# Gate weights split earlier, branch B's chunks moved to another bank ring, branch A's rings swapped

## The chip, the cores and the metric

The kernel runs on one core of a Trainium2 chip. The metric is device time in microseconds (us) of one execution; lower is better. Three runs of the kernel before gave 1930.98, 1931.53 and 1932.75 us, with a median of 1931.53 us. One further execution was taken with the hardware profiler; its own time was 1933.68 us, and the span from its first to its last instruction is 1931.9 us.

## The reference

One layer of an encoder over 1024 tokens of width 1024, all in float32:

```python
h = h + 0.5 * swiglu(rms_norm(h, ffn1_norm), ffn1_w_gate, ffn1_w_up, ffn1_w_down)
z = rms_norm(h, mix_norm) @ w_in          # 4352 columns
qa, ka, va, qb, kb, vb, ga, gb = split(z)
ya = neighbourhood_attention_2d(qa, ka, va, na_rpb)     # branch A, 8 heads
yb = windowed_gqa_sink(rope(qb), rope(kb), vb, sink)    # branch B, 8 heads on 2 key heads
merged = sigmoid(ga) * (ya @ w_branch_a) + sigmoid(gb) * (yb @ w_branch_b)
h = h + merged @ w_out
h = h + 0.5 * swiglu(rms_norm(h, ffn2_norm), ffn2_w_gate, ffn2_w_up, ffn2_w_down)
y = rms_norm(h, final_norm)
```

## The kernel before

**Arithmetic.** Every large product is made three times: each operand is split into a high part (rounded to fp32r, a cast on ScalarE, L95) and a low part (what is left, a subtraction on VectorE, L98), and TensorE adds high·high, high·low and low·high (`mm3`, L149, L151 and L153). The two feed-forward layers, most of the input projection and the output projection also use Strassen's seven products, whose combinations cost VectorE time.

**Stages in order of time.** FFN 1's hidden layer (to about 430 us), its down projection, the input projection (to about 917 us), the two attention branches with the remaining gates and the branch products in between (917 to 1207 us), the output projection (from 1207 us), and FFN 2 in the same two steps.

**PSUM.** There are eight banks of 128x512 in two rings of four, tagged `d` and `g`. `bank(tag)` takes the next free one of a ring; a matmul that opens a bank waits until the last reader of its former contents is through.

**Attention.** A loop takes 64 units (32 of branch B, then 32 of branch A), each one block of 128 queries for two heads. `scores` (L1366) takes two `d` banks, subtracts the maximum (L1382), takes the exponential (L1385) and normalises (L1389 and L1390). `turn` (L1392) transposes the probabilities on TensorE into two `d` banks (L1398) and splits them into a pair of `ws` buffers. `values` (L1405) multiplies with the values into one `g` bank, and the unit's `write` takes it out: for branch A (in `units_a`, L1340) a ScalarE copy of 64x256 (L1348), a VectorE sum of 64x256 (L1349) and two sums of 64x128 (L1352).

**What fills TensorE between units.** `filling` draws steps from a generator `filler` (L1290). Its first part is `gate` (L1197): six blocks of 128 gate columns that the projection left over (list `gates`, L945), eight steps each, two `g` banks each. The weights of a block are 512 KB, loaded and split by `load_w` (L111) at step 4 of the block before, the first block's by `gate_first` (L1102) at the end of the projection. Then comes `branch_b` (L1256): eight chunks `dc`, each four steps of `branch_mm` into two banks, whose ring alternates `d`, `g`. A chunk's gate is fetched by `fetch_gate` (L1243) into one of the two `xs` buffers one chunk ahead, opened by a tanh on ScalarE (`open_gate`, L1252), and multiplied in by VectorE (L1279), which also frees the banks. `split_y` splits the four blocks of branch B's result that the chunks multiply. Last come the first two chunks of branch A; the other six are issued by the loop after the attention, which multiplies their gates in at L1518, adds them at L1519 and forms four combinations each second chunk at L1495. `branch_a` (L1235) alternates the rings `g`, `d`, so chunk 7, the last, writes `d`. The output projection (`Down` with `n` = 4) follows on TensorE at once. Its first product P2 takes all four `d` banks at L623, and its P1 all four `g` banks at L621.

**Work behind FFN 1.** `behind_ffn1` (L739) is called after each of FFN 1's products with the number `n` of products still to come. Besides feeding the down projection, it prepares the 16 weight chunks of the two branches: `wab_fetch` (L725) loads 256 KB into a buffer of the ring `hs` (six buffers of 128x512), `wab_split` (L729, casts at L731, subtractions at L732) makes two more, and `wab_put` (L735) sends these to DRAM by POOL's queue. One chunk is taken every four products, from `n` = 80 on: fetched, split two products later, put four products later. The last put comes at `n` = 16, before the down projection uses `hs` for the bias tables.

**Key loads of branch A.** `prep_a` (L1159) is a generator drawn twice per unit that loads the queries and keys of two heads by POOL's queue, then turns the values.

**Order.** A list scheduler places the instructions of each engine; those marked `pin` keep their program order. FFN 1's first stage is ordered by hand.

Of the kernel before, what the change touches and what calls it, by code (L numbers as in the profile page):

```python
# [36 lines left out]
def trunk_kernel(ctx, tc, x, xt, n1, wg1, wu1, wd1, nm, win, rpb, sink, wa, wb, wo,  # L37
# [681 lines left out]
    wab_d = dram.tile([2 * NC8, P, 1024], F32, name="wab_d")  # L719
    cast = {}  # L720
# [4 lines left out]
    def wab_fetch(i):  # L725
        r = cast[i] = hs(F32)
        nc.sync.dma_start(r.rearrange("p (c f) -> p c f", f=P), w_cols(*((wb[0], i * P) if i < NC8 else (wa[0], a_order[i - NC8] * P))))
# [196 lines left out]
    with tc.manual_schedule(engines={E.DVE, E.Activation, E.PE, E.SP, E.Pool}):  # L924
# [17 lines left out]
    groups = [[(12, 13), (14, 15)], [(16, 17), (0, 1)], [(4, 5), (8, 9)], [(2, 3), (6, 7)], [(10, 11), (18, 19)],  # L942
              [(20, 21), (22, 23)], [(24, 25), (26, 27)]]
    NG = len(groups)
    gates = [dc for dc in [*range(8, 16), *range(8)] if 18 + dc not in sum((p for g in groups for p in g), ())]  # L945

# [154 lines left out]

    def gate_first():  # L1102
        mix["gate"] = load_w(win[0], GA + gates[0] * P, xs4())
# [55 lines left out]
    def prep_a(hp):  # L1159
# [75 lines left out]
    def branch_a(i):  # L1235

        bs = [bank("gd"[i % 2]) for _ in range(2)]
# [14 lines left out]
    def open_gate(dc):  # L1252
        r = mix["rb", dc]
        pin(nc.scalar.activation(r, r, AF.Tanh, scale=0.5))

    def branch_b():  # L1256
# [4 lines left out]
        for dc in range(NC8):  # L1261
            bs = [bank("dg"[dc % 2]) for _ in range(2)]
            mm = branch_mm(bs, mix.pop(("w", dc)), Y_B)
            for c in range(4):
                drain(mm, 1)
                yield
                if c == 0:
                    if dc == 0:
                        open_gate(0)
                    if dc + 1 < NC8:  # L1270
                        fetch_gate(dc + 1)
                elif c == 1:
# [4 lines left out]
            for n in range(2):  # L1277
                sl = slice(n * 512, (n + 1) * 512)
                nc.vector.scalar_tensor_tensor(out=merged(dc)[:, sl], in0=rb[:, sl], scalar=1.0, in1=bs[n],  # L1279
# [374 lines left out]
```

## Time and profile before

| | us |
|---|---|
| median of three runs | 1931.53 |
| lowest and highest | 1930.98, 1932.75 |
| profiled execution, its own time | 1933.68 |
| profiled execution, span | 1931.9 |
| TensorE (PE) busy in the span | 1913.6 |
| VectorE (DVE) busy | 1458.8 |
| ScalarE (ACT) busy | 947.6 |

In the profile PE stands for TensorE's matmuls, PEld for its weight loads, DVE for VectorE, ACT for ScalarE, POOL for GpSimd; SPq and POOLq are the queues that issue DMAs. L12 is line 12 of the kernel. A row of the timeline gives start, length, engine, line, operation and operands, and in brackets the idle time before it with what ended it. A row of the table by stage gives for each stretch of time the busy time and, in brackets, the number of instructions of each engine, then PEclk, the clock granted to TensorE as a share of the full one, the mean busy share of the DMA engines, and GB/s. A row of the list of waits gives who waited for whom, the total in us, the number of times and the longest. Matmuls are pipelined, so the 0.39 us of one overlaps the next; their spacing is the measure of speed.

### The profile page before, as it was taken

To read this page: it belongs to the slowest core of one execution; us is meant where nothing else is said; L and a number is where in the kernel's file an instruction comes from. 1 tells how busy PE (TensorE), PEld (TensorE's weight loads), DVE (VectorE), ACT (ScalarE), POOL (GpSimd) and SP (SyncE) were. 2 spreads that over 40 slices of the span, in tenths; PEclk is the share of its full clock that TensorE was granted. 3 is DMA by queue.
4 is the path that set the end of the run, shared out by engine and by line. 5 is a ranking of instruction groups with operands and counts; after the bars stand their busy time and mean duration, and the time that the engine had idled before them with its cause. 6 is when DMAs were issued, how large, how long until landed. Compare 5 with 4: busy or idle time off the path is not lost.

```text
span 1931.9 us, 25661 instructions
## 1 busy us (share of the span) xinstructions
PE 1913.6 (99%) x8908; PEld 1592.9 (82%) x8908; DVE 1458.8 (76%) x2559; ACT 947.6 (49%) x1846; POOL 297.4 (15%) x458
## 2 busy tenths in 40 slices
PE   9999999999999999999999999999999999999998
PEld 7888888888888888888888788788888888888886
DVE  8987766668966878656888997989676566569864
ACT  7532444444446543435898883465333333344453
POOL 0011111214400112211112101010111001005210
PEclk9999999999999999999999999999999999999999
DMA  6254555586354377834438958543422323492341
GB/s 267 94 173 166 177 177 192 171 300 241 124 172 150 108 199 239 257 107 140 128 89 216 242 198 302 175 153 120 147 96 101 130 87 105 146 353 101 113 136 67
DMA packets 161408, 321.76 MB, mean 167 GB/s; under 512 B 16384, under 2 KB 70016, under 8 KB 161280
## 3 DMA queue, kind: packets, MB, share of 16 engines
q1 hardware_dynamic: 130048, 225.21, 35.9%
q0 software_dynamic: 30512, 93.87, 14.7%
q8 instruction: 70, 1.15, 0.2%
q10 hardware_dynamic: 720, 1.05, 0.1%
q14 instruction: 58, 0.48, 0.1%
HBM read 222.04 MB, written 99.81 MB: 167 GB/s over the span
## 4 chain that ended last, share of the span: by engine, by line
PE 94%; DVE 3%; ACT 2%; issue 1%; DMA 1%; SPq 0%; POOLq 0%; POOL 0%; DVEq 0%
PE g L151 17%; PE g L149 17%; PE g L153 17%; PE d L149 12%; PE d L153 12%; PE d L151 12%; PE d L1398 2%; PE g L1417 1%; PE d L1379 1%; PE d L1380 1%; ACT fa L1385 1%; PE g L1412 1%; PE d L142 1%; ACT ws L95 1%; DVE ar L98 0%
## 5 line engine op out<-in xcount | busy, mean ns | idle before, releaser
L149 PE MATMUL g<-ar,ws 128*128 128x512 f32 x1064 | 406.8, 392 | 0.0
L151 PE MATMUL g<-ar,ws 128*128 128x512 f32 x1064 | 404.5, 390 | 0.0
L153 PE MATMUL g<-ar,ws 128*128 128x512 f32 x1064 | 404.0, 390 | 0.0
L149 PE MATMUL d<-ar,ws 128*128 128x512 f32 x784 | 303.0, 391 | 0.7 <-ACT ar L877 0.5
L151 PE MATMUL d<-ar,ws 128*128 128x512 f32 x784 | 302.0, 390 | 0.6 <-DVE ar L879 0.6
L153 PE MATMUL d<-ar,ws 128*128 128x512 f32 x784 | 301.2, 390 | 0.2 <-DVE ws L322 0.2
L153 PEld LDWEIGHTS g<-ar,ws 128*128 128x128 f32 x1064 | 199.3, 188 | 40.6
L151 PEld LDWEIGHTS g<-ar,ws 128*128 128x128 f32 x1064 | 199.4, 188 | 40.3
L322 DVE TENSOR_TENSOR ws<-raw,ws 128x512 fp32r<-128x512 f32 x222 | 152.1, 691 | 102.6 <-ACT ws L319 101.5
L149 PEld LDWEIGHTS g<-ar,ws 128*128 128x128 f32 x1064 | 197.7, 188 | 37.6 <-DVE fa L997 0.4
L319 ACT CAST ws<-raw 128x512 fp32r<-128x512 f32 x222 | 136.5, 621 | 152.2 <-PE g L153 65.0
L149 PEld LDWEIGHTS d<-ar,ws 128*128 128x128 f32 x784 | 146.9, 188 | 31.8 <-ACT ar L877 1.1
L153 PEld LDWEIGHTS d<-ar,ws 128*128 128x128 f32 x784 | 147.1, 188 | 30.9 <-DVE ws L322 0.7
L151 PEld LDWEIGHTS d<-ar,ws 128*128 128x128 f32 x784 | 147.0, 188 | 30.8 <-DVE ar L879 1.2
L95 ACT CAST ws<-raw 128x512 fp32r<-128x512 f32 (+1 forms) x103 | 66.4, 645 | 125.8 <-PE d L153 62.2
L98 DVE TENSOR_TENSOR ws<-raw,ws 128x512 fp32r<-128x512 f32 (+1 forms) x103 | 79.7, 774 | 44.3 <-ACT ws L95 44.2
L426 POOL DMA_DIRECT2D hid<-fx x91 | 49.4, 543 | 374.0 <-DVE fx L486 245.8
L98 DVE TENSOR_TENSOR ws<-ar,ws 128x512 fp32r<-128x512 f32 x114 | 93.9, 831 | 16.2 <-ACT ws L95 16.1
L95 ACT CAST ar<-raw 128x512 fp32r<-128x512 f32 (+1 forms) x81 | 54.1, 671 | 85.6 <-PE g L151 50.8
L149 PE MATMUL g<-ws,ws 128*128 128x512 f32 x232 | 90.9, 392 | 0.0
L153 PE MATMUL g<-ws,ws 128*128 128x512 f32 x232 | 90.4, 390 | 0.0
L151 PE MATMUL g<-ws,ws 128*128 128x512 f32 x232 | 90.3, 389 | 0.0
(313 smaller groups left out, 3669.8 us busy)
## 6 DMA issues: line engine op xcount, KB each, us to landing
raw<-hid SPq DMA_DIRECT2D x70, 512.0 KB
hid<-fx POOLq DMA_DIRECT2D x91, 256.0 KB, 2.6
ar<-in_ffn_w_down_dram SPq DMA_DIRECT2D x32, 512.0 KB
raw<-in_ffn_w_up_dram SPq DMA_DIRECT2D x31, 512.0 KB
raw<-in_ffn_w_gate_dram SPq DMA_DIRECT2D x27, 512.0 KB
hid<-fa POOLq DMA_DIRECT2D x51, 256.0 KB, 2.8
raw<-in_w_in_dram SPq DMA_DIRECT2D x25, 512.0 KB
ar<-zs_d POOLq DMA_DIRECT2D x48, 256.0 KB, 6.9
```

The source lines that it names most:

```text
L95: hi = nc.scalar.copy(dst_hi, src)
L98: (eng or nc.vector).tensor_tensor(dst_lo, src, f32v(dst_hi), op=ALU.subtract)
L142: nc.tensor.transpose(pt[:, c * P:(c + 1) * P], xs[:, (half * 4 + c) * P:(half * 4 + c + 1) * P], ident)
L149: nc.tensor.matmul(b, lhs[0], r[0], start=first, stop=False, **kw)
L151: nc.tensor.matmul(b, lhs[0], r[1], start=False, stop=False, **kw)
L153: nc.tensor.matmul(b, lhs[1], r[0], start=False, stop=last, **kw)
L319: nc.scalar.copy(w[0][:, :512], a)
L322: nc.vector.tensor_tensor(w[0][:, 512:], a, f32v(w[0][:, :512]), op=ALU.subtract)
L426: nc.gpsimd.dma_start(hid[PRODUCTS.index(p), i], src)
L1379: nc.tensor.matmul(b[:, :nw], un["q"][s], un["kd"][s][:, k0 * P:k1 * P], start=True, stop=False)
L1380: nc.tensor.matmul(b[:, :nw], un["q"][s], un["kl"][s][:, k0 * P:k1 * P], start=False, stop=True)
L1398: nc.tensor.transpose(pt[:, i * P:(i + 1) * P], un["pr"][s][:, i * P:(i + 1) * P], ident)
```

## The change

1. **Gate weights.** `behind_ffn1` now also fetches, splits and stores the weights of the six left-over gate blocks, as twelve half blocks of 256 KB after the sixteen branch chunks. It takes one item every three products instead of every four, from `n` = 100 on instead of 80; the split still comes two products after the fetch, the store three instead of four. In the attention `gate_load` fetches the two finished halves (high and low, 512 KB each) straight into two `ws` buffers, where `load_w` fetched 512 KB into `raw` and split it there.
2. **Branch B's chunks** all take their two banks from ring `g`, that of the values.
3. **Their gates** are fetched two chunks ahead. Chunks 0, 3 and 6 put theirs into two spare `hs` buffers (`held[4]` and `held[5]`), opened by two tanh instead of one. The split of the third block of branch B's result moves one gate step later, that of the fourth into chunk 0; chunk 0's gate is opened one step later.
4. **Branch A's rings** are swapped: chunk 0 writes `d`, chunk 7 writes `g`.
5. **Key loads**: `prep_a` yields once more for each of its two halves, between the key loads and the query loads.
6. **Branch A's write**: for the first three head pairs one 64x256 sum replaces the two 64x128 ones, with the two heads side by side in the same partitions; the store to DRAM is rearranged to match.

```diff
     def wab_fetch(i):
         r = cast[i] = hs(F32)
-        nc.sync.dma_start(r.rearrange("p (c f) -> p c f", f=P), w_cols(*((wb[0], i * P) if i < NC8 else (wa[0], a_order[i - NC8] * P))))
+        if i >= 2 * NC8:
+            k, half = divmod(i - 2 * NC8, 2)
+            src = w_cols(win[0], GA + gates[k] * P)[:, 4 * half:4 * half + 4]
+        else:
+            src = w_cols(*((wb[0], i * P) if i < NC8 else (wa[0], a_order[i - NC8] * P)))
+        nc.sync.dma_start(r.rearrange("p (c f) -> p c f", f=P), src)
     def wab_put(i):
+        g, half = divmod(i - 2 * NC8, 2)
         for k, a in enumerate(cast.pop(i)):
-            nc.gpsimd.dma_start(wab_d[i, :, k * 512:k * 512 + 512], f32v(a))
+            dst = wab_d[i, :, k * 512:k * 512 + 512] if g < 0 else wg_d[g, k, :, half * 512:half * 512 + 512]
+            nc.gpsimd.dma_start(dst, f32v(a))
     def behind_ffn1(n):
...
-        for e, f in ((4, wab_put), (2, wab_split), (0, wab_fetch)):
-            i, k = divmod(80 - e - n, 4)
-            if k == 0 and 0 <= i < 2 * NC8:
+        for e, f in ((3, wab_put), (2, wab_split), (0, wab_fetch)):
+            i, k = divmod(100 - e - n, 3)
+            if k == 0 and 0 <= i < 2 * (NC8 + len(gates)):
                 f(i)
...
+    def gate_load(k):
+        hl = [ws4() for _ in range(2)]
+        for a, src in zip(hl, (wg_d[k, 0], wg_d[k, 1])):
+            nc.sync.dma_start(f32v(a), src)
+        mix["gate"] = [a.rearrange("p (c f) -> p c f", f=P) for a in hl]
+
     def gate_first():
-        mix["gate"] = load_w(win[0], GA + gates[0] * P, xs4())
+        gate_load(0)
...
                 for a in halves(dst[k]):
                     nc.gpsimd.dma_start(a, head(k, 4, lo))
+                yield
             for lo in range(2):
                 nc.gpsimd.dma_start(halves(qs[k])[k ^ lo], head(k, 0, lo))
             yield
...
     def branch_a(i):
-        bs = [bank("gd"[i % 2]) for _ in range(2)]
+        bs = [bank("dg"[i % 2]) for _ in range(2)]
...
     def fetch_gate(dc):
-        mix["rb", dc] = xs4()
-        nc.sync.dma_start(mix["rb", dc], g_d[D + dc * P:D + (dc + 1) * P, :])
+        t = xs4() if dc % 3 else None
+        mix["rb", dc] = [held[4 + k] if t is None else t[:, k * 512:k * 512 + 512] for k in range(2)]
+        for r, cols in zip(mix["rb", dc] if t is None else [t], (slice(0, 512), slice(512, 1024)) if t is None else (slice(0, 1024),)):
+            nc.sync.dma_start(r, g_d[D + dc * P:D + (dc + 1) * P, cols])
     def open_gate(dc):
-        r = mix["rb", dc]
-        pin(nc.scalar.activation(r, r, AF.Tanh, scale=0.5))
+        for r in mix["rb", dc]:
+            pin(nc.scalar.activation(r, r, AF.Tanh, scale=0.5))
     def branch_b():
...
-            bs = [bank("dg"[dc % 2]) for _ in range(2)]
+            bs = [bank("g") for _ in range(2)]
...
-                if c == 0:
+                if c == (0 if dc else 2) and dc + 2 < NC8:
+                    fetch_gate(dc + 2)
+                if c == 0 and dc == 0:
+                    split_y(Y_B[3], 3 * P, nc.vector)
+                if c == 1:
                     if dc == 0:
                         open_gate(0)
-                    if dc + 1 < NC8:
-                        fetch_gate(dc + 1)
-                elif c == 1:
                     fetch_w(dc + 2)
...
     def filler():
...
-                yield from gate(dc, {4: lambda: mix.update(gate=load_w(win[0], GA + nxt * P))})
+                yield from gate(dc, {4: lambda: gate_load(gates.index(nxt))})
             else:
-                yield from gate(dc, {0: lambda: [fetch_y(c * P) for c in range(2)],
+                yield from gate(dc, {0: lambda: [fetch_gate(0)] + [fetch_y(c * P) for c in range(2)],
...
-                                     5: lambda: [split_y(Y_B[2], 2 * P, nc.vector), fetch_gate(0)],
-                                     6: lambda: split_y(Y_B[3], 3 * P, nc.vector)})
+                                     5: lambda: fetch_gate(1),
+                                     6: lambda: split_y(Y_B[2], 2 * P, nc.vector)})
...
     def units_a():
...
                     nc.vector.tensor_tensor(lo, o[:HD, :, 1, :], lo, op=ALU.add)
+                    cols = slice((j - 3) * P, (j + 1) * P)
+                    if hp < 3:
+                        both = y[j // 4 * HD:j // 4 * HD + HD].rearrange("p (s t) -> p s t", s=2)
+                        nc.vector.tensor_tensor(both[:, :, j % 4 * P:(j % 4 + 1) * P], o[:HD, :, 0, :], lo, op=ALU.add)
+                        if j in (3, 7):
+                            nc.gpsimd.dma_start(y_d[512 + hp * P:512 + (hp + 1) * P, cols].rearrange("(s p) t -> p s t", s=2), both)
+                        return
                     for s in range(2):
                         rows = slice(s * HD, s * HD + HD)
                         nc.vector.tensor_tensor(y[rows, j * P:(j + 1) * P], o[:HD, s, 0, :], lo[:, s, :], op=ALU.add)
-                    cols = slice((j - 3) * P, (j + 1) * P)
-                    if j in (3, 7) and hp == 3:
+                    if j in (3, 7):
                         split(slot(22)[:, cols], slot(23)[:, cols], y[:, cols])
-                    elif j in (3, 7):
-                        nc.gpsimd.dma_start(y_d[512 + hp * P:512 + (hp + 1) * P, cols], y[:, cols])
```

More of the change, by code (lines that the diff above doesn't have):

```diff
@@ L719, in trunk_kernel @@
     wab_d = dram.tile([2 * NC8, P, 1024], F32, name="wab_d")
+    groups = [[(12, 13), (14, 15)], [(16, 17), (0, 1)], [(4, 5), (8, 9)], [(2, 3), (6, 7)], [(10, 11), (18, 19)],
+              [(20, 21), (22, 23)], [(24, 25), (26, 27)]]
+    NG = len(groups)
+    gates = [dc for dc in [*range(8, 16), *range(8)] if 18 + dc not in sum((p for g in groups for p in g), ())]
+    wg_d = dram.tile([len(gates), 2, P, 1024], F32, name="wg_d")
     cast = {}
@@ L939, in trunk_kernel @@
     mix = {}
[L942 to L945, printed above, removed]
     def by_block(a):
```

2 lines of the change are left out of this document (1 added, 1 removed).

## The prediction

> **What bounds the kernel now.** First the page's own sums and the chain of work that ended last.
>
> ```profile
> span 1931.9 us, 25661 instructions
> PE 1913.6 (99%) x8908; PEld 1592.9 (82%) x8908; DVE 1458.8 (76%) x2559; ACT 947.6 (49%) x1846; POOL 297.4 (15%) x458
> PE 94%; DVE 3%; ACT 2%; issue 1%; DMA 1%; SPq 0%; POOLq 0%; POOL 0%; DVEq 0%
> ```
>
> TensorE is busy for 1913.6 of 1931.9 us, so 18.3 us of shown idle time is all that a change which leaves its matmuls alone can work on, beside places where it is busy but slow. The change adds and removes no matmul. Next, by stage: FFN 1 where the new splits go, and the attention in two parts.
>
> ```profile
> 150.00:250.00 100.00, 100.00 (x443) 82.84 (x442) 74.07 (x115) 36.80 (x62) 15.10 (x28) 1.00 0.50 168
> 250.00:350.00 100.00, 100.00 (x443) 82.83 (x442) 66.09 (x102) 41.09 (x72) 18.45 (x35) 1.00 0.55 182
> 917.00:1044.00 127.00, 126.12 (x772) 110.14 (x771) 111.59 (x365) 113.54 (x304) 21.23 (x37) 1.00 0.50 125
> 1044.00:1174.00 130.00, 125.31 (x739) 107.94 (x739) 114.54 (x353) 103.80 (x262) 17.56 (x32) 1.00 0.84 243
> ```
>
> FFN 1 shows no idle TensorE, and VectorE has 26 to 34 us per 100 to spare. The attention's first part, with the gates, loses 0.88 us of 127; its second, with branch B's chunks, 4.69 of 130. The list of TensorE's waits says for whom:
>
> ```profile
> PE d L1398 <- DVE fa L1389: 2.7, 4, 1.0
> PE d L149 <- DVE raw L1518: 2.4, 1, 2.4
> PE g L798 <- POOL ident masks.py:199: 1.5, 1, 1.5
> PE d L1379 <- DVE nmx L1382: 1.1, 3, 0.5
> PE d L1379 <- DVE ws L98: 0.8, 2, 0.4
> PE d L1185 <- DVE nmx L1382: 0.2, 1, 0.2
> ```
>
> The first is a transpose waiting for normalised probabilities: VectorE is late. The last three are matmuls that open a `d` bank whose former contents VectorE still reads, 2.1 us together. The second is one single wait of 2.4 us, so I looked at it in the timeline of TensorE.
>
> ```profile
> 1202.26 0.61 PE L149 MATMUL d<-ar,ws 128*128 128x512 f32 x2
> 1207.70 0.39 PE L149 MATMUL d<-ws,ws 128*128 128x512 f32 x1
> 1208.84 0.39 PE L153 MATMUL d<-ws,ws 128*128 128x512 f32 x1
> 1211.62 0.50 PE L149 MATMUL d<-ws,ws 128*128 128x512 f32 x1 [2.39 <-DVE raw L1518]
> 1212.99 0.63 PE L153 MATMUL d<-ws,ws 128*128 128x512 f32 x1
> 1222.91 0.39 PE L149 MATMUL g<-ar 128*128 128x512 f32 x1
> ```
>
> The last chunk of branch A runs from 1202.26 to 1207.70: 24 matmuls in 5.44 us, 0.2267 us each. Then the output projection's P2 begins, 4 entries of 12 matmuls. After six of them it needs the third `d` bank, which the last chunk has just filled. P2 should take 48 x 0.2267 = 10.88 us and end at 1218.58; P1 begins at 1222.91. The stall costs 4.33 us, not 2.4. The table of short stretches shows where the rest goes:
>
> ```profile
> 1212.00:1214.00 2.00, 2.00 (x8) 1.57 (x7) 1.93 (x3) 0.49 (x1) 0.00 (x0) 0.69 0.94 299
> 1214.00:1216.00 2.00, 2.00 (x7) 1.52 (x6) 1.98 (x5) 2.00 (x5) 0.79 (x2) 0.50 0.48 180
> 1216.00:1218.00 2.00, 2.00 (x10) 1.65 (x9) 2.00 (x5) 2.00 (x5) 0.84 (x2) 0.96 0.48 182
> ```
>
> The granted clock (the third number from the end) falls to half behind the gap. What is missing from 1.00 in the three rows is (0.31 + 0.50 + 0.04) x 2 us = 1.7 us: half speed for some 3.4 us.
>
> **Branch A's rings swapped.** With the swap P2's four `d` banks are those of chunks 4 and 6, and the last chunk sits in `g`, which is not opened before P1. VectorE's timeline at that place:
>
> ```profile
> 1207.70 1.28 DVE L1518 SCALAR_TENSOR_TENSOR raw<-raw,g 128x512 f32<-128x512 f32 x2
> 1210.88 1.28 DVE L1518 SCALAR_TENSOR_TENSOR raw<-raw,d 128x512 f32<-128x512 f32 x2
> 1212.19 1.23 DVE L1519 TENSOR_TENSOR ar<-ar,raw 128x1024 f32<-128x1024 f32 x1
> 1215.38 0.68 DVE L98 TENSOR_TENSOR ws<-ar,ws 128x512 fp32r<-128x512 f32 x1
> 1223.21 0.68 DVE L98 TENSOR_TENSOR ws<-ar,ws 128x512 fp32r<-128x512 f32 x1
> ```
>
> Before, the last chunk's `d` banks are emptied only from 1210.88 on (second row). The first row empties chunk 6's banks by 1208.98, the first of them about 0.6 us sooner; P2 wants the third bank at 1207.70 + 6 x 0.2267 = 1209.06 and the fourth at 1209.74. That suffices if VectorE keeps its order. What is late next is P2's fourth entry, whose left side is chunk 7: added up by 1213.42 (third row), split by 1216.06 (fourth row), while TensorE reaches its second matmul at 1207.70 + 37 x 0.2267 = 1216.09. So nothing is to spare there; I take 0.2 us off. Further on there is room: entry 8's last operand is there at 1223.89 (fifth row) and used at 1222.91 + 4 x 2.72 = 1233.79, ten microseconds later, so the gain isn't swallowed in the projection. Value 4.1 us, bounds 0 (the wait finds another place) and 4.3. The Trainium skill, page "TensorE: Matmul & The Clock Gate", section "HAM oscillation — how this bites in real kernels", lets the clock fall only behind idle gaps of more than some 3.4 us; by that rule a gap this short costs itself alone, 2.4 us, and the forecast below would be 1926.8 us instead of 1925.1. The trace disagrees, with 0.50 behind 2.39 us, and the trace decides.
>
> **Gate weights split behind FFN 1.** The groups of the attention that go, the two that change in the write, and the like work in FFN 1:
>
> ```profile
> L98 DVE TENSOR_TENSOR ws<-raw,ws 128x1024 fp32r<-128x1024 f32 x5 | 6.1, 1213 | 0.0
> L95 ACT CAST ws<-raw 128x1024 fp32r<-128x1024 f32 x5 | 5.2, 1049 | 0.0
> L1352 DVE TENSOR_TENSOR fa<-g,s 64x128 f32<-64x128 f32 x63 | 17.7, 281 | 0.7
> L1349 DVE TENSOR_TENSOR s<-g,s 64x256 f32<-64x256 f32 x32 | 13.1, 409 | 5.6 <-ACT s L1348 5.4
> L731 ACT CAST hs<-hs x16: 617/623/627, 218.6 to 379.1; 128x512 fp32r<-128x512 f32 x16
> L732 DVE TENSOR_TENSOR hs<-hs,hs x16: 682/687/693, 219.2 to 383.2; 128x512 fp32r<-128x512 f32 x16
> ```
>
> Added in FFN 1: 12 casts x 0.623 = 7.5 us of ScalarE, 12 subtractions x 0.687 = 8.2 us of VectorE, 12 fetches and 24 stores of 256 KB. Over the 81 products from `n` = 100 (81 x 12 x 0.2267 = 220 us) VectorE gets 8.2 us more, where it has about 66 free. Cost 0, hidden behind TensorE; without cover it would be those 8.2 us. What is queued behind the new waits is the weight loads of FFN 1 on SP and the stores of the hidden layer on POOL; both queues wait there already:
>
> ```profile
> SPq L727 <- DVE hs L732: 27.7, 6, 13.6
> POOL ar L1174 <- PE d L1380: 9.7, 2, 6.7
> ```
>
> SP stood up to 13.6 us at such a fetch (first row) and TensorE did not notice, so bounds are 0 and a few us of loss. In the attention 6.1 us of VectorE and 5.2 us of ScalarE go, all before 1044, where only 0.88 us is lost: worth 0 to 0.9, I take 0.3. The weights now come by two DMAs of 512 KB instead of one, four gate steps ahead of use; four steps are half of a gate, and the six gates fill 127 us, so some 10 us. I cost that at nothing; if it is late, five gates wait.
>
> **Branch B in ring `g`.** The 2.1 us of waits at `d` banks should mostly go, since scores, transposes and value turns have the ring to themselves: 1.6 us (bounds 0 and 2.1). In `g`, a chunk holds two of four banks, the next needs two others, and a unit's values hold one in between. No row shows a chunk change there. The nearest are the gates, which change six times in that same ring; the list of waits has none at all for a reader of a `g` bank. The far bound is the time in which a change waits for a value bank's readers, then for the pair that empties the old chunk:
>
> ```profile
> 1160.64 0.57 DVE L1352 TENSOR_TENSOR fa<-g,s 64x128 f32<-64x128 f32 x2
> 1163.99 0.37 ACT L1348 COPY s<-g 64x256 f32<-64x256 f32 x1 [1.15 <-PE g L1412]
> 1100.63 1.28 DVE L1279 SCALAR_TENSOR_TENSOR ar<-xs,g 128x512 f32<-128x512 f32 x2
> ```
>
> That is 0.37 + 0.41 (L1349 above) + 0.57 + 1.28 = 2.63 us, times 7 changes = 18.4 us. I take 0.1 us a change, 0.7 in all, nearest to the gates.
>
> **The write, the third home, the splits, the key loads.** One sum of 64x256 (0.41 us, as L1349) for two of 64x128 (0.57 a pair) saves 0.16 x 24 units = 3.8 us of VectorE, about 3 us of it where VectorE is busiest. Opening three gates in two halves costs ScalarE a few tenths each, off the path. The split moves of the third and fourth block thin the crowd of 1.2 us instructions before the scores. The 2.7 us of transposes waiting for L1389 are VectorE's lateness; I take half of what lies behind 1044, 1.1 us (bounds 0 and 2.7). The key loads' extra step lets POOL's queue wait less in one piece (9.7 us, above); behind them stand stores only. It ends a unit later than before: for the second head pair, begun at unit 33, at unit 38.5, used at unit 40. Cost 0.
>
> **The sum.** 4.1 + 0.3 + 1.6 - 0.7 + 1.1 = 6.4 us. The profiled execution took 1933.68 us by its own time, 1.8 us outside the span, and 2.15 above the median; the stalls are differences inside the span, so I take them off: 1933.68 - 6.4 = 1927.3 for an execution under the profiler, and 1931.53 - 6.4 = 1925.1 us for the median.
>
> **The rivals.**
> - **Only the swap pays.** VectorE and ScalarE stay as crowded in the second part (114.5 of 130 us busy), because what was taken off lies before 1044. For it: the stage that was relieved had nothing to lose. Against it: the write's 3 us fall right there. 1931.5 - 4.1 = 1927.4.
> - **Only the gap itself comes back.** The clock falls at this place without it too, and the swap returns 2.39 us instead of 4.1. Against: the clock stood at 1.00 up to the gap and at 0.50 behind it. 1931.5 - 6.4 + 1.7 = 1926.8. (This is what the page's rule above would make of the place.)
> - **The gap moves.** The banks of chunk 6 are emptied late: its matmuls ended at 1202.26 and VectorE came to them at 1207.70 only. If it comes 1.5 us later still, P2 stalls again, or its fourth entry does. Against: its order there was made by priorities that the swap leaves alone. 1931.5 - 2.3 = 1929.2; the swap would then not do what it does here.
> - **Everything goes.** All 5.57 us of idle time in the two attention parts and the 4.3: 1921.7.
> - **Slower: the values' ring is too small.** The chunk changes wait in `g`, in order on TensorE, with scores and transposes of the units behind them. At the far bound 18.4 - 4.1 - 1.6 = 12.7 us more than before: 1944. It cancels all other gains from (4.1 + 0.3 + 1.6 + 1.1) / 7 = 1.0 us a change, and is visible as slower from 1.6. For it: at 1100.63 VectorE empties a chunk's banks well after the chunk's end, so an old chunk can hold two banks while the new one starts. Against: the scheduler sees the ring and can put other matmuls first, and the gates lived in it.
>
> **How the numbers follow.** Forecast 1925.1: 0.41. Only the gap itself: 0.04. Only the swap: 0.16. The gap moves: 0.12. Everything goes: 0.11. Slower by the ring: 0.16. About 0.2% or 3.9 us is what a measurement tells from no change, so faster means below 1927.7, slower above 1935.4. Faster: 0.36 of the forecast's 0.41, 0.03 of the next, 0.09 of the swap alone, 0.02 of the moved gap, all 0.11 of the case in which everything goes: 0.61. Slower: of the last rival 0.11, and 0.05 for a late gate load or a queue in FFN 1 that none of the rows shows: 0.16. Same: 0.23. The range runs from 1919.5 (everything, and some of the slowness that a pipelined, busy TensorE hides) to 1934, leaving out most of the last rival; the likeliest's own is 1922 to 1929.
>
> **What would show it.** Right: no idle time at P2's third bank, a granted clock of 1.00 from 1200 to 1225, and 10.9 us from P2's first matmul to P1's; no waits of L1379 for L1382 or L98; L1352 at 64x256 for 24 units; FFN 1 without idle TensorE. Wrong: a wait of TensorE at a `g` bank for L1279 or L1352 at the chunk changes; a wait of the gates' L149 for a DMA; a clock below 1.00 behind any new gap; a P2 that stalls for chunk 6's L1518 or for its fourth entry's split.

## The result and the profile after

The changed kernel takes 1925.45 us (median of six runs, 1924.60 to 1926.82) against 1932.15 us before on the same chip (six runs, 1930.98 to 1935.34): a ratio of 0.9962, 95% interval 0.9949 to 0.9975. The profiled execution took 1925.21 us by its own time. These lines of its page are the sums of the engines:

```profile
span 1923.4 us, 25770 instructions
PE 1911.4 (99%) x8908; PEld 1592.9 (83%) x8908; DVE 1455.9 (76%) x2541; ACT 948.3 (49%) x1860; POOL 310.2 (16%) x482
```

The matmuls are the same 8908. The table by stage for the changed kernel, with the same stretches as before (FFN 1 twice, the attention's two parts, and the output projection's start):

```profile
150.00:250.00 100.00, 100.00 (x443) 82.81 (x442) 78.27 (x123) 40.08 (x69) 23.30 (x43) 1.00 0.67 231
250.00:350.00 100.00, 100.00 (x443) 82.81 (x442) 67.34 (x104) 42.71 (x75) 21.66 (x40) 1.00 0.61 203
917.00:1044.00 127.00, 126.28 (x781) 111.47 (x779) 107.05 (x360) 109.87 (x300) 21.85 (x38) 1.00 0.54 144
1044.00:1174.00 130.00, 128.04 (x748) 109.73 (x747) 113.83 (x335) 106.71 (x271) 16.72 (x31) 1.00 0.89 257
1200.00:1230.00 30.00, 30.00 (x134) 24.85 (x133) 29.84 (x48) 12.59 (x23) 3.79 (x7) 1.00 0.63 220
```

FFN 1 carries the new work (VectorE 78.27 of 100 us where it had 74.07) and TensorE still has no idle time there. The attention's first part hardly changes (0.72 us idle instead of 0.88), although VectorE has 4.5 us less to do in it. The second part loses 1.96 us instead of 4.69. In the last row TensorE is busy throughout at a granted clock of 1.00.

Where the time came from can be read off four places of TensorE's timeline: the first score, the last transpose, the first matmul of P2 and the first of P1. Before, the first two are these rows (the others are in the prediction):

```profile
915.44 0.28 PE L1379 MATMUL d<-ar,ar 128*128 128x256 f32 x1
1166.54 0.60 PE L1398 MATMUL d<-ident,fa 128*128 128x128 f32 x4
```

The same four in the changed kernel:

```profile
915.47 0.28 PE L1400 MATMUL d<-ar,ar 128*128 128x256 f32 x1
1162.45 0.60 PE L1419 MATMUL d<-ident,fa 128*128 128x128 f32 x4
1203.60 0.39 PE L149 MATMUL d<-ws,ws 128*128 128x512 f32 x1
1214.48 0.39 PE L149 MATMUL g<-ar 128*128 128x512 f32 x1
```

From first score to last transpose 251.10 us became 246.98, 4.1 less. P2 took 1222.91 - 1207.70 = 15.21 us and takes 1214.48 - 1203.60 = 10.88, 4.3 less. The two sum to 8.4 of the 8.5 us by which the spans differ; everything else is as it was. By the medians the gain is 6.7 us: the profiled execution of before was a long one, 1.5 us above its median. So the medians are the measure, and the profiles tell the places.

TensorE's waits between 900 and 1260 us, changed kernel (waiter, releaser, total, times, longest):

```profile
PE g L149 <- DVE fa L1376: 0.8, 1, 0.8
PE g L149 <- DMA ws<-wg_d: 0.4, 1, 0.4
PE g L1433 <- DVE fa L1370: 0.4, 1, 0.4
PE d L1400 <- DVE nmx L1403: 0.2, 1, 0.2
PE g L1433 <- DVE ws L98: 0.2, 1, 0.2
```

(L1400, L1403, L1410 and L1419 are before's L1379, L1382, L1389 and L1398; L1433 is L1412, L1376 is L1352, L1370 is the new single sum, L1296 is L1279, L1539 is L1518.) The transposes no longer wait for normalised probabilities, and the waits at `d` banks are down to 0.2 us. New are a wait of 0.8 us behind the last head pair's sums and one of 0.4 us for the first half of a gate's weights.

### The profile page after: what moved, and what is told of

It reads as the page before. It is cut to its first block, busy times and chain, and to the rows that moved or that the text cites. A ratio compares the mean times of both kernels' runs of the same rounds, so it can differ in the third digit from the quotient of the medians.

```text
span 1923.4 us, 25770 instructions
## 1 busy us (share of the span) xinstructions
PE 1911.4 (99%) x8908; PEld 1592.9 (83%) x8908; DVE 1455.9 (76%) x2541; ACT 948.3 (49%) x1860; POOL 310.2 (16%) x482
## 5 line engine op out<-in xcount | busy, mean ns | idle before, releaser
L149 PE MATMUL g<-ar,ws 128*128 128x512 f32 x1096 | 420.5, 393 | 1.3 <-DVE fa L1376 0.8
L151 PE MATMUL g<-ar,ws 128*128 128x512 f32 x1096 | 417.1, 390 | 0.0
L153 PE MATMUL g<-ar,ws 128*128 128x512 f32 x1096 | 415.8, 390 | 0.1
L149 PE MATMUL d<-ar,ws 128*128 128x512 f32 x752 | 291.2, 390 | 0.1
L151 PE MATMUL d<-ar,ws 128*128 128x512 f32 x752 | 290.4, 389 | 0.3 <-DVE ar L891 0.3
L153 PE MATMUL d<-ar,ws 128*128 128x512 f32 x752 | 290.2, 389 | 0.0
L153 PEld LDWEIGHTS g<-ar,ws 128*128 128x128 f32 x1096 | 205.5, 188 | 42.9 <-DMA ws<-wg_d 0.6
L151 PEld LDWEIGHTS g<-ar,ws 128*128 128x128 f32 x1096 | 205.6, 188 | 41.4 <-DVE ar L98 0.4
L149 PEld LDWEIGHTS g<-ar,ws 128*128 128x128 f32 x1096 | 203.5, 188 | 40.9 <-issue 1.2
L322 DVE TENSOR_TENSOR ws<-raw,ws 128x512 fp32r<-128x512 f32 x222 | 151.9, 690 | 94.4 <-ACT ws L319 93.5
L319 ACT CAST ws<-raw 128x512 fp32r<-128x512 f32 x222 | 136.3, 620 | 151.8 <-PE g L153 72.1
L151 PEld LDWEIGHTS d<-ar,ws 128*128 128x128 f32 x752 | 141.2, 188 | 29.9 <-DVE ar L891 0.9
L153 PEld LDWEIGHTS d<-ar,ws 128*128 128x128 f32 x752 | 141.1, 188 | 29.8 <-DVE ws L322 0.4
L149 PEld LDWEIGHTS d<-ar,ws 128*128 128x128 f32 x752 | 141.1, 188 | 29.7 <-ACT ws L319 0.5
L95 ACT CAST ws<-raw 128x512 fp32r<-128x512 f32 x98 | 61.0, 623 | 120.8 <-PE d L153 59.9
L98 DVE TENSOR_TENSOR ws<-raw,ws 128x512 fp32r<-128x512 f32 x98 | 73.0, 745 | 44.5 <-ACT ws L95 44.4
L98 DVE TENSOR_TENSOR ws<-ar,ws 128x512 fp32r<-128x512 f32 x114 | 93.7, 829 | 13.9 <-ACT ws L95 13.8
L149 PE MATMUL g<-ws,ws 128*128 128x512 f32 x232 | 90.9, 392 | 0.0
```

Of the source, the lines that this page charges most:

```text
L95: hi = nc.scalar.copy(dst_hi, src)
L98: (eng or nc.vector).tensor_tensor(dst_lo, src, f32v(dst_hi), op=ALU.subtract)
L149: nc.tensor.matmul(b, lhs[0], r[0], start=first, stop=False, **kw)
L151: nc.tensor.matmul(b, lhs[0], r[1], start=False, stop=False, **kw)
L153: nc.tensor.matmul(b, lhs[1], r[0], start=False, stop=last, **kw)
L319: nc.scalar.copy(w[0][:, :512], a)
```

## The experiments

Every kernel below computes the whole reference. Each batch ran on a chip of its own with its own runs of the kernel before, so the ratios are compared first, not the times.

The ratios need one caution. The kernel before does not lose the same in every execution. Each run has on record its mean granted clock, to three decimals: 0.998 in 24 of the 64 runs of the kernel before behind the experiments, 0.999 in the other 40. In each of the three batches the median of the former is 1.7 to 2.1 us longer (1933.44 against 1931.53 us, 1934.32 against 1932.19, 1934.18 against 1932.45). A stretch of 3.4 us at half clock, as the prediction read it from the trace, would cost 1.7 us and take 1.7 / 1930 = 0.0009 off the mean. So the clock seems to fall in some executions only; rounding hides some of the falls, as the profiled execution of before had one and is listed with 0.999. The share at 0.998 differs by batch (7 of 27, 6 of 21, 11 of 16), and this explains more of the last batch's 1934.10 us than its chip does (0.7 to 0.9 us at the same mean clock). It can move a ratio by some 1.3 us, or 0.0007, so smaller differences between ratios of different batches are not safe.

| kernel | median us | before, same chip | ratio | 95% |
|---|---|---|---|---|
| the change | 1925.45 | 1932.15 | 0.9962 | 0.9949 to 0.9975 |
| before, branch A's rings swapped | 1929.65 | 1931.99 | 0.9985 | 0.9976 to 0.9994 |
| change without that swap | 1929.07 | 1931.99 | 0.9980 | 0.9971 to 0.9988 |
| change, branch B back in `d` and `g` | 1929.40 | 1931.99 | 0.9986 | 0.9977 to 0.9994 |
| before, branch B in `g` | 1933.18 | 1932.72 | 1.0003 | 0.9994 to 1.0012 |
| before, both ring edits | 1931.11 | 1932.72 | 0.9988 | 0.9979 to 0.9997 |
| both ring edits, weights fetched first | 1927.03 | 1934.10 | 0.9966 | 0.9954 to 0.9979 |
| both ring edits, third home, moved splits | 1928.89 | 1934.10 | 0.9976 | 0.9967 to 0.9985 |
| change without the third home | 1924.83 | 1934.10 | 0.9957 | 0.9945 to 0.9969 |
| change, gate weights split late | 1925.33 | 1931.99 | 0.9963 | 0.9951 to 0.9976 |
| change, two sums in the write | 1925.61 | 1932.72 | 0.9965 | 0.9952 to 0.9977 |
| change, last head pair in other columns | 1925.36 | 1932.72 | 0.9962 | 0.9948 to 0.9975 |
| change, coarse key loads | 1926.73 | 1934.10 | 0.9964 | 0.9952 to 0.9977 |

### Branch A's swap, alone and taken back

Alone, on the kernel before:

```diff
 def branch_a(i):
-        bs = [bank("gd"[i % 2]) for _ in range(2)]
+        bs = [bank("dg"[i % 2]) for _ in range(2)]
```

> The kernel before with branch A's rings swapped and nothing else. My theory: the stall at P2's third bank goes with the slow clock behind it, 4.3 us (2.4 of gap and 1.7 of half clock and some joints), so about 0.9978 of before, 1927.8 us beside 1932.1; from P2's first matmul to P1's 10.9 us, granted clock 1.00 there; the attention as before, 251.1 us from its first score to its last transposes. Rival 'only the gap itself': 2.4 us, 1929.7, the clock still falls there. Rival 'the gap moves': at most 1 us, another wait in P2.

The ratio is 0.9985, less than half of the change's gain; 0.9978 was expected. P2 in TensorE's timeline:

```profile
1209.00 0.39 PE L149 MATMUL d<-ws,ws 128*128 128x512 f32 x1
...
1217.51 0.39 PE L149 MATMUL d<-ws,ws 128*128 128x512 f32 x1
1218.22 0.50 PE L151 MATMUL d<-ws,ws 128*128 128x512 f32 x1 [0.32 <-DVE ws L98]
...
1220.84 0.39 PE L149 MATMUL g<-ar 128*128 128x512 f32 x1
```

and VectorE's at the same place:

```profile
1209.80 1.28 DVE L1518 SCALAR_TENSOR_TENSOR raw<-raw,d 128x512 f32<-128x512 f32 x2
...
1217.47 0.69 DVE L98 TENSOR_TENSOR ws<-ar,ws 128x512 fp32r<-128x512 f32 x1
```

The stall at the third bank is gone and P2 takes 11.84 us, 3.4 less than before. But its fourth entry now stalls. Its second matmul is due at 1209.00 + 37 x 0.2267 = 1217.39, and the subtraction that makes its operand ends at 1217.47 + 0.69 = 1218.16. With what follows that costs 11.84 - 10.88 = 0.96 us. VectorE empties chunk 6's banks 0.80 us after P2's start. In the changed kernel the same two instructions stand at

```profile
1202.97 1.28 DVE L1539 SCALAR_TENSOR_TENSOR raw<-raw,d 128x512 f32<-128x512 f32 x2
...
1210.65 0.68 DVE L98 TENSOR_TENSOR ws<-ar,ws 128x512 fp32r<-128x512 f32 x1
```

that is 0.63 us ahead of P2's start, and the operand is there at 1211.33, 0.66 us before it is due (1203.60 + 8.39 = 1211.99). So how much the swap returns hangs on how far VectorE is behind at the end of branch A. The span of this kernel is only 2.1 us shorter than before, as 1.6 us were lost ahead of the attention in this one execution.

The same edit in the other direction, on the changed kernel:

```diff
 def branch_a(i):
-        bs = [bank("dg"[i % 2]) for _ in range(2)]
+        bs = [bank("gd"[i % 2]) for _ in range(2)]
```

> The changed kernel with branch A's rings as before. My theory: the gap at P2's third bank is back with half clock behind it, 4.3 us, about 1929.8 us beside 1925.5 of the changed kernel; the attention stays at 247.0 us from first score to last transposes. Rival: chunk 7 of branch A and the earlier end of the attention no longer meet there, so the gap is smaller or absent, 1925.5 to 1927.

The ratio is 0.9980 where the change has 0.9962, a difference of 3.6 us in the medians. Six of the eleven runs have 0.998 as their mean clock, with a median of 1929.3 us, and five have 0.999, with 1927.1; the eleven runs with the swap alone and the six of the change all have 0.999. The stall is back in TensorE's timeline:

```profile
1207.15 0.51 PE L149 MATMUL d<-ws,ws 128*128 128x512 f32 x1 [2.42 <-DVE raw L1539]
```

and so is the fall of the clock in the table by stage (third number from the end):

```profile
1206.00:1208.00 2.00, 0.85 (x3) 0.71 (x4) 1.97 (x4) 0.00 (x0) 0.54 (x1) 0.88 0.95 272
1208.00:1210.00 2.00, 2.00 (x6) 1.54 (x5) 1.95 (x3) 0.96 (x2) 0.03 (x1) 0.50 0.87 297
1210.00:1212.00 2.00, 2.00 (x8) 1.60 (x7) 2.00 (x4) 2.00 (x5) 1.05 (x2) 0.77 0.55 209
```

What is missing from 1.00 is (0.12 + 0.50 + 0.23) x 2 = 1.7 us, as before the change. What is left of the gain without the swap, 1932 x 0.0020 = 3.9 us, is nearly the 4.1 us by which the attention is shorter in the changed kernel's profile.

### Branch B's ring, taken back and alone

On the changed kernel, `branch_b` alone goes back:

```diff
-            bs = [bank("g") for _ in range(2)]
+            bs = [bank("dg"[dc % 2]) for _ in range(2)]
```

> The changed kernel with branch B's chunks alternating between d and g again. My theory: scores wait for d banks again, 1.6 to 2.1 us in L1400 for L1403 or L98, the attention 248.6 to 249.1 us from first score to last transposes, 1927.3 us in all. Rival 'the gain in the attention came from VectorE alone': no change, 247.0 and 1925.5. Rival 'g had become too small': faster than the changed kernel by up to 1 us, since the wait of 0.8 us at a g bank goes.

The ratio is 0.9986, and in the profile first score to last transpose takes 251.0 us, the whole 4.1 us lost where about half was expected. P2 takes 12.06 us, 1.2 more than in the changed kernel. TensorE's waits in this kernel:

```profile
PE d L1400 <- DVE nmx L1403: 2.0, 4, 0.9
PE d L1419 <- DVE fa L1410: 1.6, 2, 1.0
PE g L153 <- DMA ws<-wg_d: 0.9, 1, 0.9
PE d L1400 <- DVE ws L98: 0.7, 2, 0.4
```

Scores wait for a `d` bank again (2.0 + 0.7 us), and transposes for normalised probabilities (1.6). Without this edit, the early splits, the third home, the single sum and the finer key loads together gain nothing in the attention.

Alone, on the kernel before, the edit is the same one reversed.

> The kernel before with branch B's chunks in g and nothing else. Theory: the attention is 4 us shorter, 247 us; the gap at P2's third bank stays with its half clock, P2 15.2 us; 1928 to 1929 us in all. Rival: TensorE waits at g banks instead, attention 250 us or more, 1931.

The ratio is 1.0003: nothing, where an attention 4 us shorter was expected. TensorE's waits say why:

```profile
PE d L149 <- DVE raw L1518: 2.7, 1, 2.7
PE g L149 <- DMA ws<-wab_d: 1.7, 1, 1.7
PE d L1379 <- DVE nmx L1382: 1.0, 2, 0.6
PE d L1398 <- DVE fa L1389: 0.8, 2, 0.4
```

The transposes' wait for L1389 falls from 2.7 to 0.8 us with this one edit (another entry, for L98, adds 0.3), so more than half of it goes with the shared ring, while VectorE's load is the same. But a chunk now waits 1.7 us for its weights. SyncE's queue shows where these stood:

```profile
1100.52 0.32 SPq L1245 DMA_DIRECT2D xs<-g_d  x1
1101.26 0.32 SPq L1249 DMA_DIRECT2D ws<-wab_d  x1
```

The fetch of the next chunk's gate (first row) goes into an `xs` buffer that an earlier chunk's L1279 has to free first; in the queue's own waits between 1040 and 1180 us that is its second longest:

```profile
SPq L1245 <- DVE ar L1279: 23.6, 4, 13.0
```

The weights (second row) come behind it in program order, and so leave late, though their own buffer need not be the one that is waited for. TensorE gets them at 1108.27, where its row shows the 1.71 us. The length of the queue's wait alone says little: the kernel before and the changed kernel stand at the gate fetch for 30.8 and 24.7 us without a chunk that waits for its weights. The list has no entry of a chunk that waits for L1279, that is for a bank of the chunk before it.

Both ring edits together, on the kernel before:

> The kernel before with its two ring lines alone changed: branch B's chunks in g, branch A's rings swapped. Theory 'the two rings are the whole gain': attention 247 us from first score to last transposes, P2 10.9 us, 1925.5 us in all, as the changed kernel. Rival 'the rest is needed too' (gates split early, third home, one sum for two): half of the attention's 4 us stays, 1927 to 1928 us. Rival 'values' ring too small without the rest': 1929 or more, with waits of TensorE at g banks.

The ratio is 0.9988, about what the swap alone gives, so the two rings are not the whole gain. There is again one wait of 1.6 us at the start of the same chunk (L149 at 1107.17), here put down to `PE g L149 <- DVE s L1349`, the reader of a value bank in `g`. By this entry alone the ring could be at fault and not the weights; the next test decides. P2 takes 11.66 us. The eleven times of this kernel spread from 1927.72 to 1932.93 us, and its profiled execution (1928.87) is one of the quicker, so its profile shows less than the median lost. Four of the six longer ones, from 1931.11 us on, have a mean clock of 0.998 or 0.997, all five quicker ones 0.999: the clock seems to fall in some executions of this kernel too, at a place that no trace shows.

### What takes the wait for the weights away

If the weights stand behind the gate's fetch, then exchanging the two in each chunk, on top of both ring edits, must help:

```diff
                 if c == 0:
                     if dc == 0:
                         open_gate(0)
-                    if dc + 1 < NC8:
-                        fetch_gate(dc + 1)
-                elif c == 1:
                     fetch_w(dc + 2)
+                elif c == 1:
+                    if dc + 1 < NC8:
+                        fetch_gate(dc + 1)
```

> The kernel before with both ring edits, and in each chunk the weights' fetch put on SP's queue one step ahead of the gate's fetch, where it was one step behind. Theory (weights stuck behind a gate fetch): the wait of 1.6 us for the weights goes, about 1.6 us faster than with the rings alone, 1929.4 us beside 1931.1. Rival: the gates come later instead and VectorE multiplies later, no change or slower, 1931 us or more.

It does: the ratio is 0.9966, most of the change's gain, with three edits of a line or two. That is more than the 1.6 us expected; by the medians it is 4.1 us, on another chip. The profiled executions of the two kernels differ by less: first score to last transpose is 1.1 us shorter and P2 0.8 us. The rest lies in the longer executions of the kernel with the rings alone and in the other chip's runs of before, and its cause isn't shown. TensorE's waits in this kernel have no entry for a DMA any more:

```profile
PE d L1398 <- DVE fa L1389: 1.0, 3, 0.4
PE d L1379 <- DVE nmx L1382: 1.0, 2, 0.6
PE d L1398 <- DVE fx L98: 0.3, 1, 0.3
```

The queue's wait for L1279 at the gate fetch is 7.2 us instead of 22.6 with the two ring edits alone (another 10.0 us there are for L1388), and P2 takes 10.88 us without a stall.

The changed kernel's own way is the third home. On top of both ring edits, with the fetches two chunks ahead and the moved splits, but with the gate weights split late, two sums in the write and the coarse key loads:

```diff
     def fetch_gate(dc):
-        mix["rb", dc] = xs4()
-        nc.sync.dma_start(mix["rb", dc], g_d[D + dc * P:D + (dc + 1) * P, :])
+        t = xs4() if dc % 3 else None
+        mix["rb", dc] = [held[4 + k] if t is None else t[:, k * 512:k * 512 + 512] for k in range(2)]
...
```

> The kernel before with both ring edits, the third home for branch B's gates (two chunks ahead) and the moved splits, and without the early gate split, the single sum and the finer key loads. Theory 'rings and home are the whole': 1925.5 us, attention 247 to 248 us. Rival 'each of the three others carries some': 1927 to 1928 us.

0.9976, between the ring edits alone and the change. The wait for a chunk's weights is 0.4 us instead of 1.6; the transposes wait 2.1 us (two entries, L1411 and L98), so VectorE is behind here as it is not in the changed kernel.

And the third home taken out of the changed kernel, with gates one chunk ahead in `xs` and the splits in their old places:

```diff
     def fetch_gate(dc):
-        t = xs4() if dc % 3 else None
-        mix["rb", dc] = [held[4 + k] if t is None else t[:, k * 512:k * 512 + 512] for k in range(2)]
...
+        mix["rb", dc] = xs4()
+        nc.sync.dma_start(mix["rb", dc], g_d[D + dc * P:D + (dc + 1) * P, :])
```

> The changed kernel with the gates of branch B fetched one chunk ahead into the two xs buffers and the splits of branch B's result where they were before; rings, gate weights, sums and key loads as changed. Theory: SP's queue, in order, stands at a gate fetch until a chunk's VectorE multiply frees an xs buffer, and the next chunk's weights wait behind it, so TensorE waits for them by 1.5 to 1.8 us in one place as in the kernel with rings only: attention 249.5 to 250.5 us, 1928.5 to 1930 us in all. Rival: the early gate split and the one sum relieve VectorE enough that the buffers come free in time: 1926 us.

This is a miss: 0.9957, not slower than the change. The wait that I had looked for came only in part, `PE g L149 <- DMA ws<-wab_d: 0.9, 1, 0.9`, and cost nothing that shows. So the third home is not needed once the other edits are there. The ratio is a little below the change's, but the intervals overlap over most of their length, so it isn't shown to be the better kernel.

### The other edits, one at a time out of the changed kernel

The gate weights split late, as before (in the attention, 16 items every four products from `n` = 80):

```diff
-            i, k = divmod(100 - e - n, 3)
-            if k == 0 and 0 <= i < 2 * (NC8 + len(gates)):
+            i, k = divmod(80 - e - n, 4)
+            if k == 0 and 0 <= i < 2 * NC8:
...
-                yield from gate(dc, {4: lambda: gate_load(gates.index(nxt))})
+                yield from gate(dc, {4: lambda: mix.update(gate=load_w(win[0], GA + nxt * P))})
```

> The changed kernel with the gate weights loaded and split in the attention, and the period of four products from n = 80, as before. My theory: the splits lie where TensorE lost 0.9 us in all, so 0.3 to 0.9 us slower in the first part of the attention, 1926 us. Rival: 11 us of work on VectorE and ScalarE push everything behind them, 2 to 4 us slower, 1928 to 1929. Rival: faster by 0.4 us, since no gate waits for its DMA.

0.9963, no difference. VectorE is busy 111.21 us in 917 to 1044 instead of 107.05, and the time doesn't show it; first score to last transpose is 0.9 us longer in the profiled execution, but begins 0.7 us earlier.

The write with two sums of 64x128 for all head pairs:

```diff
-                    if hp < 3:
+                    if False:
...
-                    if j in (3, 7):
+                    if j in (3, 7) and hp == 3:
...
```

> The changed kernel with the two 64x128 sums of before for all head pairs. Theory: VectorE gets 3.8 us more, TensorE waits for it a little more, but the wait of 0.8 us at a g bank, which comes from a sum held up by a store, goes: 0 to 1 us slower, 1925.5 to 1926.5. Rival 'VectorE bounds the second part': 2.7 us slower, 1928. Rival: faster by the 0.8 us, 1924.7.

0.9965, no difference that can be told. VectorE is busy 2.2 us more in the second part (116.06), and TensorE's waits in this kernel begin with two of transposes (L1421 and L1412 are the changed kernel's L1419 and L1410):

```profile
PE d L1421 <- DVE fa L1412: 1.0, 1, 1.0
PE d L1421 <- DVE fx L98: 0.9, 1, 0.9
```

but the wait of 0.8 us behind L1376 is gone, and first score to last transpose takes 247.15 us against 246.98.

That wait of 0.8 us is a cost of the single sum. VectorE's timeline in the changed kernel:

```profile
1135.88 0.28 DVE L1376 TENSOR_TENSOR fa<-g,s 64x128 f32<-64x128 f32 x1 [1.02 <-DMA y_d<-fa]
```

The last head pair writes its sums in the old layout into the buffer from which the store of the third pair still reads. Giving its first four units other columns takes the cause away:

```diff
-                    y = fa[:, 3072:4096]
+                    y = fa[:, 3072:4096] if hp < 3 or j > 3 else fa[:, :1024]
```

> The changed kernel, in which the last head pair's first four units write their result to a free part of fa instead of the buffer that the pair before is still being stored from. Theory: the sum held up 1.0 us by that store, and TensorE's 0.8 us behind it, go: 1924.7 us. Rival: the wait is hidden elsewhere, 1925.5.

0.9962: the wait is gone from the list and the time is the same. TensorE had 128.64 us of work in 1044 to 1174 instead of 128.04, but lost 0.2 us more ahead of that stretch, and first score to last transpose takes 247.10 us.

The key loads without the extra step:

```diff
                     nc.gpsimd.dma_start(a, head(k, 4, lo))
-                yield
```

> The changed kernel with the key loads of branch A yielding once for each half as before. Theory: only stores stand behind them on POOL's queue, no change, 1925.5 us. Rival: their transfers come in a lump and hold up others, 1926 to 1927 us.

0.9964, no difference by the ratio. The median is 1.3 us above the change's, on another chip, where the kernel without the third home took 1924.83 us; so a loss of about 1 us isn't ruled out. The profile shows 1.5 us behind L1376's sums (L1375 here) instead of 0.8, and a longer wait for gate weights (0.9); the attention takes 248.3 us and P2 11.66 in this execution, which was the longest of its five (1927.52).

## Why the prediction was right, and where its steps failed

**The total.** 6.4 us were forecast, 6.7 measured by the medians. That they lie so close is in part luck: the swap's term came out, but the terms behind it were wrong one by one, and 1.7 us of the swap's 4.1 are lost in some executions of the kernel before only. The cases "only the swap pays" and "the values' ring is too small" fell: without the swap 0.9980 remains, and the two waits for readers of a `g` bank in the changed kernel make 1.2 us, not 18.4.

**The swap, 4.1 us.** Right in mechanism: 4.3 us inside P2 in the profile, 3.6 by the medians when it is taken back, 2.3 when it is made alone. The size is that of an execution in which the clock falls. On the chip where both were run, the kernel with the swap alone is 3.8 us quicker than the runs of before at 0.998 and 1.9 us quicker than those at 0.999. The rival "only the gap itself comes back" thus holds in part: the clock does fall behind the gap, but by the mean clocks not in every execution, and the one trace could not show that. The step "nothing to spare there; I take 0.2 us off" was mis-sized. The fourth entry costs 0.96 us with the swap alone, as the rival "the gap moves" had it for one of its two places, and nothing in the changed kernel, where VectorE comes to P2's start 1.4 us earlier relative to TensorE. The prediction added the swap as a term of its own; in fact 1 us of it depends on the attention's edits.

**Gate weights, 0.3 us, and the cover of FFN 1.** The cover was right: no idle time in FFN 1. In the attention the test could not tell the edit from nothing. A late gate load, put at nothing, did appear, which was a sign of being wrong: TensorE waits for one 0.4 us in the changed kernel and 0.9 us with the coarse key loads.

**Branch B in `g`, 1.6 - 0.7 us, and VectorE's lateness, 1.1.** Here the steps failed, though their sum with the 0.3 (2.3 us) lies near what the medians leave after the swap (6.7 - 3.6 = 3.1; in the profiles it is 4.1). Three things were wrong:
- The transposes' wait was put down to VectorE's load. The ring alone takes it from 2.7 to 1.1 us in all, and it stays at 1.3 where the exchanged fetches leave no wait for weights in which VectorE could catch up. So more than half of it belonged to the ring's term. The load has a share too: two sums instead of one put 1.9 us of such waits back, though not into the time, and with the third home on the two rings they are 2.1 us.
- The price of the ring was looked for in its banks, 0.1 us at each chunk change. There it is one wait of 0.8 us for a value bank, another sign of being wrong that appeared; it is caused by the store of the third head pair, and taking it away moves no time. The price of the ring alone lies in the queue of loads, where the prediction put none: the weights behind the gate fetch come late, once, 1.7 us.
- The terms were added. The ring alone is worth 0 (1.0003), and without it the other edits leave 0.9986, the swap's worth. It is the necessary part, and it pays with help: from the exchanged fetches, in part from the third home, or from the early splits, the single sum and the finer key loads together. In the changed kernel each of its helpers can be taken out without a loss that the ratio shows.

**The third home and the key loads, cost 0.** Right for the third home in the changed kernel; for the key loads the ratio agrees, within the 1 us left open above. That each is worth 0 when removed doesn't mean that it is worth 0 when added: with the two rings the third home and the moved splits bring 0.9988 to 0.9976.

**Shown and open.** Shown are the swap's stall with its clock, the necessity of branch B's ring, and that exchanging the two fetches takes away the wait for the weights. How much of the way from 0.9988 to 0.9966 comes from that wait is open. How the rest is shared among the helpers was tried only by taking out single ones; the early splits, the single sum and the key loads were not added one at a time to the two rings. The traces show one execution of each kernel; that the clock falls in some executions only is read from mean clocks, which don't say where it fell.

## What to carry to other kernels

Where a stage opens a PSUM ring from which VectorE still has to read the last results, let the producer end in the other ring; the stall is one long entry in the list of waits, and its full price is in the spacing of the matmuls behind it, where the clock may have fallen. One trace does not say how often it falls, so look at the mean clock of all runs. Move whatever competes with the critical loop out of its ring, then look at once at the in-order DMA queue, for a load that waits for a buffer holds up the loads behind it. Where edits share buffers and queues, test each both alone and taken out: here the decisive one was worth nothing alone, and its helpers nothing when taken out singly.

## What the runs showed of the hardware

The clock does not go by the length of the gap alone. It fell to half behind 2.39 us (before) and 2.42 us (the change without the swap), each time for 1.7 / 0.5 = 3.4 us. In the kernel before with only branch B in `g` the same gap was longer, 2.74 us, and the clock stayed whole; TensorE's row and the table by stage of that kernel:

```profile
1211.97 0.50 PE L149 MATMUL d<-ws,ws 128*128 128x512 f32 x1 [2.74 <-DVE raw L1518]
```

```profile
1210.00:1212.00 2.00, 0.03 (x1) 0.03 (x1) 1.97 (x4) 0.00 (x0) 0.39 (x1) 1.00 0.80 250
1212.00:1214.00 2.00, 2.00 (x9) 1.65 (x10) 1.93 (x3) 0.14 (x1) 0.15 (x1) 1.00 0.96 227
1214.00:1216.00 2.00, 2.00 (x11) 1.65 (x10) 1.98 (x4) 2.00 (x5) 0.54 (x1) 1.00 0.61 244
```

P2 took 13.92 us there, 1.3 less than before, with a longer stall. The Trainium skill, page "TensorE: Matmul & The Clock Gate", section "What's actually happening", has the clock decided over windows of 3413 ns that run freely, whatever the kernel does. The length of the half-clock stretch agrees, and a gap that lies in one window or across two could make this difference.

Where the windows lay can be worked out: if they run freely, all falls of one trace lie on the same grid, and in every trace the clock falls once more after the last matmul. The row of before and that of the kernel with branch B in `g`:

```profile
1929.00:1930.00 1.00, 0.00 (x0) 0.00 (x0) 0.00 (x0) 0.00 (x0) 0.00 (x0) 0.77 1.01 387
1927.00:1928.00 1.00, 0.00 (x0) 0.00 (x0) 0.00 (x0) 0.00 (x0) 0.00 (x0) 0.90 0.70 270
```

In before the two falls are at 1214 - 0.62 / 0.5 = 1212.76 and 1930 - 0.23 / 0.5 = 1929.54. They are 716.78 us apart, which is 210 windows of 3.413 us, an estimate with the Trainium skill's length. The window that ends at 1212.76 began at 1209.35, and TensorE was idle from 1209.23 to 1211.62: 2.27 us in one window. Without the swap the fall is at 1208 - 0.24 / 0.5 = 1207.52, and the gap, from 1204.73 to 1207.15, lies in one window whole: 2.42 us. In the third kernel the last fall is at 1928 - 0.10 / 0.5 = 1927.80, and 716.78 us earlier, at 1211.02, a window ends inside the gap. That leaves 1.79 us idle in one window and 0.95 in the next, and the clock stayed whole. Laid on its grid in the same way, each of the fourteen traces agrees: every window with 2.27 us or more without a matmul is followed by a fall, and none with 1.79 us or less is. Where between the two it begins was not measured. Windows that run freely would also explain why the clock falls in some executions only; this is argued, not shown. The bound of some 3.4 us of idle time, which the prediction quoted from the Trainium skill and set against the trace, is about 1 us too high here.
